# A hybrid convolution and pooling layer on one core: 32 rows moved ahead of a late product, one more pair by seven products, small products in twos, loads of the gate stage reordered

## The chip, the cores and the metric

The kernel runs on one core of a Trainium2 chip. The metric is device microseconds (us) of one execution; a result is the median of several runs. Where a profile is shown, it is of one more execution, whose own time stands beside it.

## The reference

One layer of a streaming encoder (`DEPTH` is 1) works on 2048 prompt frames of one stream and on 32 sample frames that continue another, each of 1024 numbers:

```python
hn = rmsnorm(h, g_mix)
hA, bA, cA, zA, vB, zB = split(hn @ w_in)            # six groups of 512 columns
u = cA * hA
yA = bA * (causal width-3 convolution of u + conv_b) * silu(zA)
pooled = trailing mean over 2, 4, 8 or 16 frames of vB, minus vB
yB = (pooled @ pool_w, per group of 128) * pool_scale * silu(zB)
h = h + concat(yA, yB) @ w_out
gate = sigmoid(rmsnorm(h, g_ple) @ w_ple_gate)
h = h + (p @ w_ple) * gate
return rmsnorm(h, g_final), ...                      # and the states that end each stream
```

All inputs are float32. `w_in` is 1024x3072, `w_out` and `w_ple_gate` are 1024x1024, `p` has 256 numbers a frame. The sample frames take the stream's cached states as history.

## The kernel before

**Products.** Every large operand is split in two parts, a rounded one and the rest (`split`, L81 on ScalarE and L84 on VectorE), and a product takes three matmuls for each of its contraction blocks. The three large matrix products are done as a 2x2 scheme with seven block products in place of eight: the sources of one side are summed to `11`, `12`, `S1` to `S4`, `22`, those of the other to `11`, `21`, `T1` to `T4`, `22`. One block product is 12 matmuls of 128x512 on TensorE (PE). Its banks in PSUM are named `x`, `y` and `z`: `x` gathers the products `11`, `S2`, `S3` and, as the last, the one with `T4`. `carry` copies a bank's state between, `out` adds it to the result.

**First stage: units.** The projection runs in two groups (`gi`) of two blocks of 512 frames, and four units (`j`) of 128 columns of each of the six kinds. The first unit is `Unit.plain`: it does all six kinds block by block, with whole projections (`project`, L646) of 24 matmuls for a kind and a block. While it runs, the frames of the group are normalised, turned and summed (`second`, `frame_sums`), and the seven forms are split. Six are kept in SBUF as `B0`. The seventh, `T4`, has its place in a ring of one buffer (`seventh`) that is used for something else before; so its four parts are stored to DRAM as `p_d` (`to_memory`, L546), and it is loaded back after the first unit (L1290). The other seven units (`Unit.seven`) each run three pairs of kinds, (zb, v), (c, h), (za, b), by `pair`: it takes its weights from `pair_weights`, which sums and splits them product by product, and does the seven products with `half_product`. Between the products of a unit one step of an `aside` is taken: in the first group the frame sums of the next group, in the second group the turning of `p` (`turn_p`), the 32 sample frames (`new_frames`) and the weights of the embedding (`ple_weights`). `new_frames` goes through 24 parts of `w_in`, loads two ahead, and takes one part a step: 8 matmuls of 128x256 with 32 rows (L1147).

**Second stage: output rows.** Products `p @ w_ple` of the first tiles (`embed`, tile `e`) fill the time until the weights are there. Then `w_out` is applied to pairs of tiles of 128 rows, `o0`, `o2` to `o14`, by `seven`, whose steps 1 to 6 between the products run other work: in `o0` the table `LATER` prepares the late weights (`T3`, `21`, `22`, `T4`) and frames. `h_ops` (L1315) adds the rows of `x`; `done_h` stores the sum as `h_d` and takes its squares. The 32 sample rows are a tile of their own, done by `plain` with its packed products (L337, L340), named `ol`. They stand behind `o4`. `scale_gate` scales the gate's weights on the way.

**Third stage: gate.** The rest of the embedding (`rest_e`, with frames `pps` that `load_pps` loads) runs first, with the preparation of the first pair `prep_g(0)` as steps. Then pairs `g0` to `g12` and `last_pair` (14) run by `seven`. `prep_g(i)` gives two steps that prepare the pair `i` inside the pair before. `first` loads the upper tile by rows and the lower tile by quarters (`by_quarters`, L1541) and transposes the latter on VectorE (`turned_here`, L1547). `second` transposes the upper tile on PE (`turned`: copies `ho` by ScalarE at L1530, transposes `pth` at L1532), then sums and splits. `gate_ops` (L1558 to L1570) copies, adds, takes the sigmoid and updates `h`. `done_g` (L1577, L1578) scales the finished rows and stores them.

**Order.** A planner puts each engine's instructions in order beforehand, by its own estimate of when operands and buffers are there, and each engine then runs its list in that order. `keep_in_program_order` (also `in_turn`, `pin`) holds an instruction at its place in the source; `issue_after` holds a load behind another instruction. Loads and stores are issued by SP, GpSimd (POOL) and ScalarE, each in order, so a load that waits for a buffer holds up those behind it in its queue.

Of the kernel before, what the change touches and what calls it, by code (L numbers as in the profile page):

```python
# [9 lines left out]
F32 = mybir.dt.float32  # L10
F32R = mybir.dt.float32r
# [4 lines left out]
P = 128  # L16
# [20 lines left out]
def trunk(ctx, tc, x_p, x_s, c_conv, c_pool, p_p, p_s, g_mix, w_in, conv_w, conv_b, pool_w,  # L37
# [361 lines left out]
    with ExitStack() as s1:  # L399
# [197 lines left out]
        def pair_weights(gi, ka, kb, j, name, ring, s_ring, ring_b, pin):  # L597
# [17 lines left out]
            else:  # L615
# [220 lines left out]
        class Unit:  # L836
# [65 lines left out]
            def plain(self):  # L902
# [29 lines left out]
                for b in blocks:  # L932
# [3 lines left out]
                    if b:  # L936
                        next(second)
                wza = weights("za", j, f"za{tag}")
                for b in blocks:
                    z = self.cols(V, b)  # L940
                    nc.scalar.activation(z, product_of("za", b, wza), AF.Silu)
                    c = self.cols(c_s, b)
                    nc.vector.tensor_tensor(c, c, z, op=ALU.mult)
                    if b:
                        next(second)
                wb = weights("b", j, f"b{tag}")
                for b in blocks:
                    ps = product_of("b", b, wb)
                    y = self.cols(c_s, b)
                    nc.vector.tensor_tensor(y, ps, y, op=ALU.mult)  # L950
                    self.store(j, b, c_s)


            def pair(self, ka, kb, B, D, done, ring, s_ring=None, pin=False):
# [6 lines left out]
                make = pair_weights(self.gi, ka, kb, self.j, name, ring, s_ring, pool_ring if ka == "zb" else ring, pin)  # L961
                yield
# [9 lines left out]
                half_product(X, make("11"), B["11"], True)  # L972
# [21 lines left out]
            def seven(self, B, aside, both=False):  # L994
# [27 lines left out]
                za = [self.cols(V, b) for b in range(2)]  # L1022
                gb = self.cols(U, 0)

                def za_done(b):
                    nc.scalar.activation(za[b], za[b], AF.Silu)
                    mul(self.cols(c_s, b), self.cols(c_s, b), za[b])

                def b_second():
                    mul(self.cols(c_s, 1), self.cols(c_s, 1), gb)  # L1030
                    self.store(j, 1, c_s)

                def b_first(ps):
                    mul(self.cols(c_s, 0), ps, self.cols(c_s, 0))
                    self.store(j, 0, c_s)

# [6 lines left out]
                    ("za", "b", B, {(0, 0): za[0], (0, 1): za[1], (1, 1): gb},  # L1043
                     {(0, 0): lambda ps: za_done(0), (0, 1): lambda ps: (za_done(1), b_second()), (1, 1): nothing,
                      (1, 0): b_first})]
# [67 lines left out]
        def new_frames():  # L1113
# [186 lines left out]
    with ExitStack() as s2:  # L1300
# [118 lines left out]
        W["21"] = halves(seventh("wo_21"))  # L1419

# [11 lines left out]
        hold = []  # L1432

# [34 lines left out]
        for i in range(0, NT - 1, 2):  # L1468
# [365 lines left out]
```

## Time and profile before

| | us |
|---|---|
| runs | 932.33, 930.13, 931.91 (median 931.91) |
| the profiled execution | 929.11 |
| its span, first to last instruction | 927.3 |
| PE busy | 902.0 (97%) |
| VectorE (DVE) busy | 697.1 (75%) |
| ScalarE (ACT) busy | 458.5 (49%) |
| GpSimd (POOL) busy | 158.9 (17%) |
| mean granted clock of TensorE | 0.994 |

The stages, by PE's timeline: the first unit until 90, the other units until 531.7, the first embedding until 550.9, the output tiles until 716.2, the second embedding until 742.6, the gate's pairs until 917.8, and then the last rows until the end.

How the rows are read: a timeline's row has its start in the span, its length, the engine, the line of the source, the operation, the tiles written and read, shapes, and how often it stands there in a row; in brackets the engine's idle time before it and what ended that. A row of windows has the busy time and the instructions of PE, its weight loads, DVE, ACT and POOL, then the granted clock, the busy share of the DMA engines and GB/s. A row of DMA issues has the queue, the count, the size of one and the median us from issue to landing. Matmuls overlap, so a row of several ends a little after the next one begins; the distance of starts is the pace.

### The profile page before, as it was taken

How to read it: one execution, taken by the hardware profiler on the slowest of the kernel's cores; microseconds unless marked ns; L12 is line 12 of the kernel's file. 1: busy time of each engine (PE TensorE's matmuls, PEld its weight loads, DVE VectorE, ACT ScalarE, POOL GpSimd, SP SyncE). 2: the span in 40 equal slices, each digit the busy share in tenths (PEclk: the TensorE clock that was granted, in tenths of full speed). 3: DMA queues.
4: the chain of work that ended last, by engine and by line, in shares of the span. 5: the costliest groups of instructions: out<-in, count | busy, mean ns of one | idle time of the engine just before them, and what ended most of it. 6: DMA issues, size and time to landing. Idle time of an engine off the chain costs nothing. (4 is left out here: it accounts for less than half of the span.)

```text
span 927.3 us, 12203 instructions
## 1 busy us (share of the span) xinstructions
PE 902.0 (97%) x4186; PEld 723.5 (78%) x4186; DVE 697.1 (75%) x1148; ACT 458.5 (49%) x828; POOL 158.9 (17%) x309
## 2 busy tenths in 40 slices
PE   8999999999999999999999998999999999999995
PEld 6788888878888788766688886878888778778885
DVE  6895789797993687746668679765655988888884
ACT  7752555465453354523344376434434965555553
POOL 2200121122121122100010021111111311121212
PEclk9999999999999999999999999999999999999998
DMA  8164396747599675777743695867768876476652
GB/s 277 47 206 169 104 270 188 227 153 235 174 339 428 165 226 177 246 219 236 235 145 131 225 320 166 264 224 238 223 220 276 306 249 193 165 227 206 218 186 105
DMA packets 113243, 199.56 MB, mean 215 GB/s; under 512 B 13206, under 2 KB 69950, under 8 KB 112157
## 3 DMA queue, kind: packets, MB, share of 16 engines
q1 hardware_dynamic: 88733, 117.19, 40.4%
q0 software_dynamic: 22000, 77.21, 24.6%
q10 hardware_dynamic: 2448, 4.39, 1.3%
q8 instruction: 33, 0.54, 0.2%
q14 instruction: 29, 0.24, 0.1%
HBM read 133.06 MB, written 65.67 MB: 214 GB/s over the span
## 5 line engine op out<-in xcount | busy, mean ns | idle before, releaser
L185 PE MATMUL x_o<-wo,y 128*128 128x512 f32 x192 | 47.1, 400 | 3.4 <-DVE x L1315 3.4
L185 PE MATMUL z_g<-wg,g_S 128*128 128x512 f32 x192 | 47.4, 393 | 0.7 <-ACT c_g L1558 0.7
L185 PE MATMUL z_o<-wo,y_S 128*128 128x512 f32 x192 | 47.4, 389 | 0.0
L185 PEld LDWEIGHTS x_o<-wo,y 128*128 128x128 f32 x192 | 37.1, 194 | 11.8 <-issue 3.8
L185 PE MATMUL x_o<-wo_T,y_S 128*128 128x512 f32 x192 | 46.2, 390 | 0.0
L185 PEld LDWEIGHTS z_g<-wg,g_S 128*128 128x128 f32 x192 | 35.5, 188 | 8.5 <-ACT c_g L1558 1.3
L646 PE MATMUL z_ch<-B,w_ch_S 128*128 128x512 f32 x168 | 40.8, 392 | 1.2 <-ACT U L966 1.2
L185 PEld LDWEIGHTS z_o<-wo,y_S 128*128 128x128 f32 x192 | 36.0, 188 | 7.5
L185 PEld LDWEIGHTS x_o<-wo_T,y_S 128*128 128x128 f32 x192 | 35.9, 188 | 7.6 <-DVE c_o L1315 0.2
L646 PE MATMUL x_ch<-B,w_ch_S 128*128 128x512 f32 x168 | 41.8, 392 | 0.0
L646 PE MATMUL x_zab<-B,w_zab_S 128*128 128x512 f32 x168 | 40.9, 392 | 0.2 <-DVE w_zab_S L84 0.2
L646 PE MATMUL z_zab<-B,w_zab_S 128*128 128x512 f32 x168 | 41.1, 392 | 0.0
L646 PE MATMUL x_zbv<-B,w_zbv_S 128*128 128x512 f32 x168 | 40.8, 391 | 0.0
L646 PE MATMUL z_zbv<-B,w_zbv_S 128*128 128x512 f32 x168 | 40.7, 391 | 0.0
L646 PEld LDWEIGHTS z_ch<-B,w_ch_S 128*128 128x128 f32 x168 | 31.3, 188 | 8.9 <-ACT U L966 1.6
L646 PEld LDWEIGHTS x_zab<-B,w_zab_S 128*128 128x128 f32 x168 | 31.3, 188 | 7.9 <-issue 0.8
L646 PEld LDWEIGHTS x_zbv<-B,w_zbv_S 128*128 128x128 f32 x168 | 31.3, 188 | 7.7 <-issue 0.8
L646 PEld LDWEIGHTS z_zab<-B,w_zab_S 128*128 128x128 f32 x168 | 31.2, 188 | 7.5 <-issue 0.8
L646 PEld LDWEIGHTS x_ch<-B,w_ch_S 128*128 128x128 f32 x168 | 31.3, 188 | 7.3 <-issue 0.8
L646 PEld LDWEIGHTS z_zbv<-B,w_zbv_S 128*128 128x128 f32 x168 | 31.3, 188 | 7.2 <-issue 0.8
L1577 DVE SCALAR_TENSOR_TENSOR h<-h,rstd_f,g_bc 128x1024 f32<-128x1024 f32 (+1 forms) x15 | 19.3, 1284 | 14.6 <-POOL rstd_f L77 13.0
L94 ACT ACTIVATE junk<-x 128x1024 bf16<-128x1024 f32 (+1 forms) x17 | 18.0, 1056 | 22.6 <-DVE x L1315 21.1
(561 smaller groups left out, 2297.9 us busy)
## 6 DMA issues: line engine op xcount, KB each, us to landing
wn<-in_w_in_dram SPq DMA_DIRECT2D x24, 512.0 KB, 3.8
p_dT<-T POOLq DMA_DIRECT2D x16, 512.0 KB, 5.2
y<-y_d SPq DMA_DIRECT2D x16, 512.0 KB, 5.9
h<-h_d POOLq DMA_DIRECT2D x16, 512.0 KB, 5.1
e<-e_d SPq DMA_DIRECT2D x15, 512.0 KB, 4.7
x<-in_x_prompt_dram SPq DMA_DIRECT2D x14, 512.0 KB, 4.0
out_dram<-h POOLq DMA_DIRECT2D x14, 512.0 KB, 3.4
B<-p_d POOLq DMA_DIRECT2D x3, 2048.0 KB, 15.7
```

Source lines behind the costliest of these rows:

```text
L94: ins = nc.scalar.activation(junk[:n], x[:n], AF.Square, accum_out=ssq[:n])
L185: nc.tensor.matmul(ps[:n], lhs[:, k, a, :n], w[b][:, k], start=start and k + q == 0, stop=k == KH - 1 and q == 2, skip_group_check=True)
L646: nc.tensor.matmul(ps, lhs[:, k, x], b[:, k, y], start=start and k + q == 0, stop=stop and k == KH - 1 and q == 2, skip_group_check=True)
L1577: nc.vector.scalar_tensor_tensor(h[:n], h[:n], rf[:n], g_bc[:n], op0=ALU.mult, op1=ALU.mult)
```

## The change

It has these parts:

- *The first unit's third pair.* `Unit.plain` does (za, b) by `pair`, with the sums of the group's frames, in place of four whole projections. The part that tells what is done with the results is now `third`. `T4` is loaded by POOL right after `h`. `pair_weights` stores the sums of the first group's other units for the second group, as before, and none for this unit.
- *The new rows.* `new_frames` loads four parts ahead, waits two steps longer, and takes two parts every second step.
- *The 32 output rows.* `ol` runs at step 6 of `o0`, ahead of the product with `T4`; its frames (`short_y`) and rows (`short_x`) are loaded before `o0`.
- *The gate stage.* The quarters of tile 1 (`first_lower`) are loaded before the embedding's weights; the first two `pps` use another ring (`ss`); the first pair's transpose on VectorE is pinned (its steps stay behind the same embedding tiles); `second` of the pairs 2 and 8 runs a step later; loads of `h` and stores of finished rows go to SP's queue from tile 6 on, and in the last pair.

```diff
@@ pair_weights
-                if gi == 0:
+                if gi == 0 and j:
                     kept[ka, j] = k1, k3 = ...
@@ Unit.plain
                     self.conv(b)
-                    if b:
-                        next(second)
-                wza = weights("za", j, f"za{tag}")
-                for b in blocks:
-                    z = self.cols(V, b)
-                    nc.scalar.activation(z, product_of("za", b, wza), AF.Silu)
...
-                wb = weights("b", j, f"b{tag}")
-                for b in blocks:
-                    ps = product_of("b", b, wb)
...
+                    if b == 0:
+                        steps = self.pair(*self.third(B0), raw_ring, None, True)
+                        next(steps)
+                    next(second)
+                B0["T4"] = piece_of(seventh("B0_T4"), 0)
+                nc.gpsimd.dma_start(B0["T4"].bitcast(F32), p_d["T4"])
+                p_d["T4"] = tc.dram_tile([P, KH, 2, NB], F32, name="p_dT4b")
+                for _ in steps:
+                    pass
+
+            def third(self, B):
...
+                return ("za", "b", B, {(0, 0): za[0], (0, 1): za[1], (1, 1): gb},
+                        {(0, 0): lambda ps: za_done(0), (0, 1): lambda ps: (za_done(1), b_second()), (1, 1): lambda ps: None,
+                         (1, 0): b_first})
@@ Unit.pair
+                upper = make("11") if pin and self.gi == 0 else None
                 yield
...
-                half_product(X, make("11"), B["11"], True)
+                half_product(X, upper or make("11"), B["11"], True)
@@ new_frames
-            loaded = [load(0), load(1)]
+            loaded = [load(i) for i in range(4)]
+            yield
+            yield
             yield
...
-                if i + 2 < len(order):
-                    loaded.append(load(i + 2))
+                if i % 2 == 0:
+                    continue
+                loaded.extend(load(n) for n in (i + 3, i + 4) if n < len(order))
...
+                yield
                 yield
@@ units
                     u.plain()
-                    B0["T4"] = piece_of(seventh("B0_T4"), 0)
-                    nc.sync.dma_start(B0["T4"].bitcast(F32), p_d["T4"])
-                    p_d["T4"] = tc.dram_tile([P, KH, 2, NB], F32, name="p_dT4b")
@@ output rows
+        short_y = qa.tile([P, KC, DEC], F32, tag="q", name="short_y")
+        with tc.issue_after(loaded[0]):
+            nc.sync.dma_start(short_y, y_d[:, :, SEQ:].rearrange("k p t -> p k t"))
...
+        short_a = short("yl", (short_y[:, :KH], short_y[:, KH:]), DEC)
...
+        def short_tile():
+            plain("ol", short_a, W, last_n, *h_ops([short_x], last_n, "ol", two=True))
+
-        LATER = {1: third, 2: left, 3: right, 4: later("T4", 2)}
+        LATER = {1: third, 2: left, 3: right, 4: later("T4", 2), 6: short_tile}
+        short_x = load_rows(xh, "x", NT - 1, x_p, x_s)
...
-            last = i == 4
-            if last:
-                n = tiles[NT - 1][1]
-                A = short("yl", load_y(NT - 1, n), n)
+            if i == 0:
+                done_h(NT - 1, short_x)
...
-            if last:
-                x = load_rows(xh, "x", NT - 1, x_p, x_s)
-                plain("ol", A, W, n, *h_ops([x], n, "ol", two=True))
-                done_h(NT - 1, x)
@@ gate stage
+        first_lower = by_quarters(1)
...
-        got = {0: load_pps(st.tile([P, 2, 2, P], F32R, tag="t", name=f"pps_{EARLY}"), EARLY, nc.sync)}
+        got = {0: load_pps(ss.tile([P, 2, 2, P], F32R, tag="s", name=f"pps_{EARLY}"), EARLY, nc.sync)}
...
-        got[1] = st.tile([P, 2, 2, P], F32R, tag="t", name=f"pps_{EARLY + 1}")
+        got[1] = ss.tile([P, 2, 2, P], F32R, tag="s", name=f"pps_{EARLY + 1}")
...
+        def turned_here(t, pin=False):
+            ins = nc.vector.transpose(t, t)
+            if pin:
+                tc.keep_in_program_order(ins)
...
-            nc.gpsimd.dma_start(rows_of(y_p, y_s, r, n), h[:n])
+            (nc.sync if 6 <= i < NT - 1 else nc.gpsimd).dma_start(rows_of(y_p, y_s, r, n), h[:n])
@@ last_pair
-            h = [load_rows(xh, "h", i + b, h_d, queue=nc.gpsimd) for b in range(2)]
+            h = [load_rows(xh, "h", i + b, h_d) for b in range(2)]
...
-                (nc.scalar if b else nc.gpsimd).dma_start(y[:, cut:], o[:, cut:])
+                (nc.scalar if b else nc.sync).dma_start(y[:, cut:], o[:, cut:])
@@ prep_g and the loop over the gate's pairs
-                got["lower"] = by_quarters(i + 1)
+                got["lower"] = by_quarters(i + 1) if i else first_lower
...
-            return {2: first, 3: second}
+            return {2: first, 4 if i in (2, 8) else 3: second}
...
-                steps[2 if c == 2 else 3]()
+                steps[c // 2 + 1]()
...
-            h = [load_rows(xh, "h", i + b, h_d, queue=nc.gpsimd) for b in range(2)]
+            h = [load_rows(xh, "h", i + b, h_d, queue=nc.gpsimd if i < 6 else nc.sync) for b in range(2)]
```

More of the change, by code (lines that the diff above doesn't have):

```diff
@@ L1498, in trunk, with by_quarters @@
         weight_parts(W, tops, None, "11", "T1")
+        def by_quarters(i):
+            r, n = tiles[i]
+            t = ring4(ya, f"hn_{i}")
+            for q in range(4):
+                nc.sync.dma_start(t[q * 32:q * 32 + 32].rearrange("p (g c) -> p g c", g=4),
+                                  h_d[r:r + P, q * 256:q * 256 + 256].rearrange("(g p) c -> p g c", p=32))
+            return t
+        first_lower = by_quarters(1)
         shared = slot("wq")
         wp = [[shared[:, (2 * k + h) * D:(2 * k + h + 1) * D] for h in range(2)] for k in range(2)]
-        got = {0: load_pps(st.tile([P, 2, 2, P], F32R, tag="t", name=f"pps_{EARLY}"), EARLY, nc.sync)}
+        got = {0: load_pps(ss.tile([P, 2, 2, P], F32R, tag="s", name=f"pps_{EARLY}"), EARLY, nc.sync)}
         for k in range(2):
@@ L1534, in turned @@
             return out
-        def by_quarters(i):
-            r, n = tiles[i]
-            t = ring4(ya, f"hn_{i}")
-            for q in range(4):
-                nc.sync.dma_start(t[q * 32:q * 32 + 32].rearrange("p (g c) -> p g c", g=4),
-                                  h_d[r:r + P, q * 256:q * 256 + 256].rearrange("(g p) c -> p g c", p=32))
-            return t
-        def turned_here(t):
-            nc.vector.transpose(t, t)
+        def turned_here(t, pin=False):
+            ins = nc.vector.transpose(t, t)
+            if pin:
+                tc.keep_in_program_order(ins)
             u = t.rearrange("p (g k t) -> p k g t", g=4, k=KC)
@@ L1742, in first @@
                     load()
-                lower.extend(turned_here(got["lower"]))
+                lower.extend(turned_here(got["lower"], not i))
             def second():
```

36 lines of the change are left out of this document (15 added, 21 removed).

## The prediction

> **What bounds the kernel now.** First I read the page's busy shares, then the list of what TensorE (PE) waits for, then PE's timeline around each place that the change touches, each time with the other engines' timelines beside it.
>
> ```profile
> PE 902.0 (97%) x4186; PEld 723.5 (78%) x4186; DVE 697.1 (75%) x1148; ACT 458.5 (49%) x828; POOL 158.9 (17%) x309
> ```
>
> PE works 902.0 of the span's 927.3 us. So time goes only where PE has fewer matmuls, runs them faster, or waits less. The single largest wait inside it is this:
>
> ```profile
> PE x_o L185 <- DVE x L1315: 3.4, 1, 3.4
> ...
> PE pth L1532 <- ACT ho L1530: 1.8, 2, 1.2
> PE e L109 <- DMA pps<-pp_d: 1.6, 1, 1.6
> ```
>
> (the columns are total, times, longest). The change works on all three of these and takes matmuls away in two places. I cost its four parts in order of time. The profiled execution took 929.11 us, 2.80 under the median of the runs (931.91); the parts are summed against the profile, and the sum is then taken from the median.
>
> **Part A: the first unit's third pair by seven products.** Before, `za` and `b` are four full projections of 24 matmuls:
>
> ```profile
> 68.22 11.04 PE L646 MATMUL za<-B,w_za 128*128 128x512 f32 x48
> 79.10 11.04 PE L646 MATMUL b<-B,w_b 128*128 128x512 f32 x48
> 89.98 2.88 PE L646 MATMUL x_zbv<-B,w_zbv 128*128 128x512 f32 x12
> ```
>
> From 68.22 to 89.98 stand 96 matmuls in 21.76 us, 0.2267 each (a product of 12 is 2.72). Seven products are 84: −2.72. The weight sums that this adds are DVE's, which has room there (third busy column):
>
> ```profile
> 80.00:84.00 4.00, 4.00 (x19) 3.32 (x18) 2.65 (x5) 0.41 (x1) 0.00 (x0) 1.00 0.29 109
> 84.00:88.00 4.00, 4.00 (x20) 3.30 (x19) 0.69 (x1) 0.54 (x1) 0.00 (x0) 1.00 0.24 88
> ```
>
> In the changed order only the second product's weights come late, by an estimated 0.2 from the number of pieces (0.6 to 0.7 each) ahead of them in DVE's queue.
>
> The new wait is the seventh product's frames, `T4`. They are split, stored to DRAM by POOL in four parts, and loaded back as one. Before, the load was needed only by the next unit's seventh product; now PE wants it after 72 of the pair's matmuls and 2 of the next unit, at 68.22 + 74 × 0.2267 + 0.2 = 85.2.
>
> ```profile
> 71.28 0.68 DVE L84 TENSOR_TENSOR T<-f,T 128x512 fp32r<-128x512 f32 x1
> ```
>
> ```profile
> 72.25 0.84 POOL L546 DMA_DIRECT2D p_dT<-T  x1 [9.63 <-DVE T L84]
> ```
>
> ```profile
> B_T<-p_dT SPq DMA_DIRECT2D x1, 2048.0 KB, 8.5
> ...
> p_dT<-T POOLq DMA_DIRECT2D x1, 512.0 KB, 4.2
> ```
>
> ```profile
> B<-p_d POOLq DMA_DIRECT2D x3, 2048.0 KB, 15.7
> ```
>
> The last part is stored at 72.25, right behind its split. In the changed order two more splits stand ahead of it on DVE (0.6 each by the steps of that queue), so the store goes out at 73.45 and lands at 77.65 (4.2). The load then takes 8.5 by the row of the same load before; the other row, 15.7, is of 2 MB loads that were queued seven at once on POOL, and is the far end. So `T4` lands at 86.2, and PE waits 1.0 (bounds: 0, and 93.4 − 85.2 = 8.2). I take 8.5, because it is the same transfer at nearly the same time. A = −2.72 + 0.2 + 1.0 = −1.5; the bounds are −2.5 and +5.7, or +7.6 with the slow clock that part B shows behind a long wait. The Trainium skill's "DMA: Bandwidth & Descriptors" (section "Anatomy of one DMA — SWDGE (gpsimd) path") fits such a transfer as 2.0 us plus bytes over 436 GB/s, an estimate of 6.8 for 2 MB, with which there would be no wait and the sum would be 1.0 better; no row here shows a 2 MB load that fast.
>
> **Part B: the 32 rows before the late product.** The short tile stood behind `o4`; now it stands inside `o0`, before the product of `A22` with `T4`.
>
> ```profile
> 567.50 0.61 PE L185 MATMUL x_o<-wo,y 128*128 128x512 f32 x2
> 571.53 6.88 PE L185 MATMUL x_o<-wo,y 128*128 128x512 f32 x22 [3.42 <-DVE x L1315]
> ```
>
> ```profile
> 570.71 0.68 DVE L1315 TENSOR_TENSOR x<-x_o,x 128x512 f32<-128x512 f32 x1
> ```
>
> ```profile
> 572.00:574.00 2.00, 2.00 (x6) 1.54 (x6) 2.00 (x4) 0.72 (x1) 0.52 (x1) 0.55 0.87 203
> 574.00:576.00 2.00, 2.00 (x7) 1.54 (x6) 1.84 (x4) 1.93 (x5) 1.08 (x2) 0.59 0.97 274
> ```
>
> ```profile
> 722.00:726.00 4.00, 2.42 (x15) 1.91 (x14) 3.93 (x8) 4.00 (x10) 2.09 (x3) 1.00 1.00 379
> ```
>
> PE does two matmuls of the next tile and then waits for DVE to empty the bank (done at 571.39). Behind the wait the granted clock (the third number from the end) is 0.55 and 0.59, with 6 and 7 matmuls in 2 us where 0.2267 each makes 9. The last row is a stretch with a shorter wait, of 1.57 (part D): its clock is 1.00. The 24 matmuls from 567.50 end at 571.53 + 6.71 = 578.24: 10.74 where 24 × 0.2267 = 5.44 are due, so 5.30 are lost, 3.42 waiting and the rest to the clock. The Trainium skill's "TensorE: Matmul & The Clock Gate" (Part 1) says that a window of about 3.4 us idle halves the clock until one such window was busy: with that a stall well under 3.4 costs only itself. The trace agrees on both sides, half the clock after 3.42 and all of it after 1.57; so I price short stalls at their length, and long ones like this one.
>
> ```profile
> 613.66 1.08 PE L337 MATMUL x_ol<-wo,yl_a 128*64 128x512 f32 x4
> ...
> 621.02 1.32 PE L185 MATMUL x_o<-wo,y 128*128 128x512 f32 x5
> ```
>
> The short tile costs 7.36 in either place. In the changed order 24 of its 32 matmuls (5.5 us) stand between `S4` and the late product, which PE so reaches at 573.0. DVE gets to the sum at 571.39 plus two small splits of the short rows (0.5): 571.9, 1.1 early. The short tile's last eight matmuls wait for a DVE sum that I place at 574.3, when PE is there at 574.4. Its frames are loaded behind the lower weight rows and split by DVE some 10 us after, and the load of `o2`'s rows, which now waits for a store of `o0`'s rows, has some 5 us in hand; these are estimates from the queues' orders and the durations of such rows. B = −5.3, −5.1 with 0.2 for that tight step; if DVE were late by its own queue, part of the 3.42 would stay, so −3 at the worst.
>
> **Part C: the new rows' products two at a time.** 24 groups of 8 small matmuls stand between the big products of the second half. Before, most stand alone:
>
> ```profile
> 396.05 1.07 PE L1147 MATMUL new<-wn,xs 128*32 128x256 f32 x16
> 397.05 3.06 PE L646 MATMUL x_zbv<-B,w_zbv 128*128 128x512 f32 x12
> 400.04 0.64 PE L1147 MATMUL new<-wn,xs 128*32 128x256 f32 x8
> 400.60 3.02 PE L646 MATMUL y_zbv<-B,w_zbv 128*128 128x512 f32 x12
> 403.56 0.64 PE L1147 MATMUL new<-wn,xs 128*32 128x256 f32 x8
> ```
>
> A pair of groups and a product take 400.04 − 396.05 = 3.99, so the pair costs 1.27; a single and a product take 403.56 − 400.04 = 3.52, so the single costs 0.80. Before there are 18 singles and 3 pairs, 18.2 us; the changed order has 12 pairs, 15.2. C = −3.0, and I see no reason for a gain beyond it; if the saving came only from the switch at one side, half would be left (−1.5).
>
> ```profile
> wn<-in_w_in_dram SPq DMA_DIRECT2D x24, 512.0 KB, 3.8
> ```
>
> The weight rows (3.8 us to land) are now loaded four ahead and two per two steps, so each has over 6 us. The steps behind them move by two products, 5.4 us; what they make is used only by the embedding, when the units are over: hidden.
>
> **Part D: the gate stage.** Loads are moved ahead, so PE's wait for the embedding's frames goes:
>
> ```profile
> 724.30 16.60 PE L109 MATMUL e<-wq,pps 128*128 128x512 f32 x72 [1.57 <-DMA pps<-pp_d]
> ...
> 752.15 1.18 PE L1532 MATMUL pth<-ident,ho 128*128 128x128 f32 x8 [1.22 <-ACT ho L1530]
> ...
> 759.52 3.01 PE L185 MATMUL z_g<-wg,g_S 128*128 128x512 f32 x12 [0.73 <-ACT c_g L1558]
> ```
>
> ```profile
> 751.48 1.14 ACT L1530 COPY ho<-hn 128x512 f32<-128x512 f32 x2 [4.01 <-DMA hn<-h_d]
> ```
>
> −1.6 in the embedding. Then `g0` has less room. Before, ACT waited 4.01 for the upper rows of the next pair, and PE lost 1.22 + 0.73 = 1.95. In the changed ACT order the copies of these rows stand ahead of the copy that frees `g0`'s first bank for the third product. That product ended at 752.15 − 1.22 = 750.9, so it began at 748.2, and would begin at 746.6 now that PE is 1.6 earlier. If the rows land as late as before (751.48), PE waits 6 us with the copies. The quarters of the lower tile are loaded earlier, so less is ahead of these rows; I place the landing in the middle, at 748, and with the two copies (1.14) and the bank's (0.5) the wait is 3.0 against 1.95: +1.0 (bounds −2 and +4). The second wait on `ho` (1.8 − 1.2 = 0.6 in the list above) goes with the transposes moved by a step, and I give back half for new tight places: −0.3. D = −1.6 + 1.0 − 0.3 = −0.9.
>
> The later pairs take a new risk. From tile 6 on, the output stores go to SP's queue, which issues in order, and there they stand ahead of the load of the next upper rows. That load so waits for DVE's last scaling:
>
> ```profile
> 860.93 1.28 DVE L1577 SCALAR_TENSOR_TENSOR h<-h,rstd_f,g_bc 128x1024 f32<-128x1024 f32 x1 [0.71 <-POOL rstd_f L77]
> ```
>
> ```profile
> 864.87 1.18 PE L1532 MATMUL pth<-ident,ho 128*128 128x128 f32 x8
> ```
>
> ```profile
> e<-e_d SPq DMA_DIRECT2D x5, 512.0 KB, 5.9
> ```
>
> By these times the store goes at 862.2, the load at 862.8, lands by 5.9 at 868.7, and the copy ends 0.57 later, at 869.3. PE's transposes stood at 864.87; the changed order has them later by half a product and 11 matmuls, at 864.87 + 1.36 + 2.49 = 868.7. So 0 to 0.6 in each of two pairs; I take none of it for the sum.
>
> **The sum.** −1.5 − 5.1 − 3.0 − 0.9 = −10.5: 918.6 for an execution like the profiled one, and 931.91 − 10.5 = 921.4 for the median.
>
> **The rivals.**
> - *T4 lands late* (0.12). For it: 2 MB loads took 15.7. Against: that was a queue of seven. A then is +7.6 instead of −1.5, 930.5 in all.
> - *The upper rows behind the stores come late, no slow clock* (0.12). Two pairs lose some 1.7 each where the load takes 7 instead of 5.9: 924.8. For it: the load is the first that waits for this scaling. Against: the transposes were moved back with it.
> - *The same with the slow clock, slower than before* (0.07). If in `g6`, `g8` and `g10` the rows come over 3.4 us late, each costs what part B's wait cost, 5.3 less 0.2: 921.4 + 15.3 = 936.7. This decides from a landing of about 9 us; the 5.9 above is against it, the DMA share of 1.00 at 722 (the last number but one of that row) is for it, if the pairs see such a load again.
> - *T4 in time and `g0` without a new wait* (0.07): 1.0 + 2.0 better, 918.4; for it, DMA is at 0.24 to 0.29 of its share from 80 to 88, against it, it is the 8.5 of the one row. The skill's figure for a load would give the first of these.
> - *It does not do what it says*: the built program shows the order of its instructions, seven products and twelve pairs among them, so only times are open.
>
> **How the numbers follow.** The forecast holds 0.62, with 917.5 to 925 as its own range. With the cases beside it the range is 917.5 to 928.5; outside lie the slower case, half of the late `T4`, and a little at the low end. About 0.3% (2.8 us) is what a measurement of this kernel can tell from no change: the bounds are 929.1 and 934.7. Faster: 0.62 + 0.12 + 0.07 + half of 0.12 = 0.87; same: the other half, 0.06; slower: 0.07.
>
> **What would show it.** A: PE's `x_zab` product with `T4` right behind `z_zab`, with a wait near 1. B: no wait on x_o, the clock at 1.00 from 564 to 580. C: 12 rows of 16 `new` matmuls. D: no wait on `pps`, and a wait of some 3 in `g0`'s first block. I am wrong if the waits on `B_T`, `ho` or `hn` sum to more than 8 us, or if B's lost 5.3 reappears at another product of `o0` or `o2`.

## The result, and the profile after

The changed kernel took 920.0 us (median of 4 runs, 917.26 to 922.09) against 932.12 for the kernel before (930.13 to 932.85): a ratio of 0.9872, with a 95% interval of 0.9839 to 0.9904. The forecast was 921.4 with a range of 917.5 to 928.5, so the time is right. The profiled execution took 917.26, the fastest of the four, with a span of 915.5, and it shows that two of the four terms were not: A brought nothing, and D far more than its 0.9.

The page's busy shares, and then the list of PE's waits, of the changed kernel:

```profile
PE 895.3 (98%) x4174; PEld 722.7 (79%) x4174; DVE 702.6 (77%) x1158; ACT 460.3 (50%) x834; POOL 151.6 (17%) x291
```

```profile
PE gm L447 <- DMA gm_row<-in_g_mix_dram: 2.3, 1, 2.3
PE x_zab L646 <- DMA B_T<-p_dT: 2.3, 1, 2.3
PE e L109 <- DMA wq<-wl_d: 1.6, 1, 1.6
```

PE has 12 matmuls less, and 6.7 us less of busy time. The wait on `x_o` is gone from the list, and so are both on `ho`. In their place stands a wait of 2.3 on `T4` (`B_T`), and the wait at the second embedding is as long as before but on another transfer: `wq`, not `pps` (in eight other profiles with the same loads at this place it was shorter, 0.3 to 1.2).

The stages tell more than the list. From the starts of the same products in both timelines of PE:

| stretch | before | after | difference | predicted |
|---|---|---|---|---|
| start to the first unit's third pair | 68.22 | 68.75 | +0.5 | 0 |
| that pair, and the next unit's first product (A) | 24.48 | 24.45 | 0.0 | −1.5 |
| units from there to the new rows | 296.28 | 297.46 | +1.2 | 0 |
| new rows, to the units' end (C) | 142.73 | 139.64 | −3.1 | −3.0 |
| first embedding | 19.19 | 19.20 | 0.0 | 0 |
| output tiles (B) | 165.34 | 160.48 | −4.9 | −5.1 |
| second embedding (D) | 26.34 | 26.43 | +0.1 | −1.6 |
| `g0`, to `g2`'s second product (D) | 25.24 | 22.70 | −2.5 | +1.0 |
| later pairs, to the last embedding (D) | 143.98 | 142.70 | −1.3 | −0.3 |
| to the last matmul's end | 5.94 | 5.95 | 0.0 | 0 |
| from there to the end of the span (D) | 9.56 | 7.74 | −1.8 | 0 |

B and C are as worked out. In B the short tile stands where the wait stood, and PE's timeline runs through:

```profile
566.56 1.08 PE L337 MATMUL x_ol<-wo,yl_a 128*64 128x512 f32 x4
...
572.09 1.54 PE L185 MATMUL x_o<-wo,y 128*128 128x512 f32 x6
573.47 1.08 PE L337 MATMUL x_ol<-wo,yl_a 128*64 128x512 f32 x4
574.39 1.09 PE L340 MATMUL x_ol<-wo,yl_a 128*32 128x512 f32 x4
575.31 4.26 PE L185 MATMUL x_o<-wo,y 128*128 128x512 f32 x18
```

From 566.56 to 572.09 are the 5.53 that cover DVE's sum, and PE goes on without a wait; the clock is 1.00 in all windows from 564 to 580, of which this is one (busy time and count of PE, PEld, DVE, ACT, POOL, then clock, DMA share, GB/s):

```profile
572.00:576.00 4.00, 4.00 (x19) 2.71 (x18) 3.88 (x7) 1.15 (x2) 1.35 (x2) 1.00 0.89 274
```

For C, two rows of the same timeline:

```profile
396.93 1.07 PE L1149 MATMUL new<-wn,xs 128*32 128x256 f32 x16
...
403.64 1.07 PE L1149 MATMUL new<-wn,xs 128*32 128x256 f32 x16
```

A pair and two products take 403.64 − 396.93 = 6.71, which is 1.27 for the pair. The prediction's 1.27 held to the digit, and 12 such rows stand in the timeline.

In A the wait is there, more than twice as long as priced:

```profile
85.22 0.61 PE L646 MATMUL x_zbv<-B,w_zbv 128*128 128x512 f32 x2
88.11 2.98 PE L646 MATMUL x_zab<-B_T,w_zab 128*128 128x512 f32 x12 [2.28 <-DMA B_T<-p_dT]
```

and so the 2.7 us of twelve matmuls are given back on the spot.

### The profile page after: what moved, and what is told of

It reads as the page before. It is cut to its first block, busy times and chain, and to the rows that moved or that the text cites. A ratio compares the mean times of both kernels' runs of the same rounds, so it can differ in the third digit from the quotient of the medians.

```text
span 915.5 us, 12179 instructions
## 1 busy us (share of the span) xinstructions
PE 895.3 (98%) x4174; PEld 722.7 (79%) x4174; DVE 702.6 (77%) x1158; ACT 460.3 (50%) x834; POOL 151.6 (17%) x291
## 4 chain that ended last, share of the span: by engine, by line
PE 65%; DMA 7%; issue 5%; DVE 2%; ACT 1%; POOL 1%; SPq 0%; POOLq 0%; DVEq 0%; ACTq 0%
PE x_g L185 9%; PE x_o L185 9%; PE x_zab L646 5%; PE z_g L185 5%; PE e L109 4%; PE x_zbv L646 4%; PE x_ch L646 4%; PE z_o L185 4%; DMA raw_zab_0b<-in_w_in_dram 4%; PE z_zab L646 2%; PE y_g L185 2%; PE y_o L185 2%; PE z_ch L646 2%; PE z_zbv L646 2%; DMA B<-p_d 2%
## 5 line engine op out<-in xcount | busy, mean ns | idle before, releaser
L646 PE MATMUL x_zab<-B,w_zab_S 128*128 128x512 f32 x192 | 46.9, 392 | 0.6 <-ACT V L983 0.4
L646 PE MATMUL z_zab<-B,w_zab_S 128*128 128x512 f32 x192 | 46.7, 390 | 0.0
L185 PE MATMUL x_o<-wo,y 128*128 128x512 f32 x192 | 45.2, 389 | 0.0
L646 PEld LDWEIGHTS x_zab<-B,w_zab_S 128*128 128x128 f32 x192 | 35.7, 188 | 9.6 <-ACT V L983 0.8
L646 PEld LDWEIGHTS z_zab<-B,w_zab_S 128*128 128x128 f32 x192 | 35.8, 188 | 7.8 <-DVE w_zab_S L84 0.3
L81 ACT CAST y_S<-y_fS 128x512 fp32r<-128x512 f32 x28 | 17.0, 620 | 27.2 <-PE x_o L185 11.5
L1316 DVE TENSOR_TENSOR c_o<-x_o,x 128x512 f32<-128x512 f32 x14 | 9.7, 690 | 21.9 <-PE x_o L185 21.8
```

The costliest lines, as they stand in the source:

```text
L81: ins = nc.scalar.copy(hi, src)
L185: nc.tensor.matmul(ps[:n], lhs[:, k, a, :n], w[b][:, k], start=start and k + q == 0, stop=k == KH - 1 and q == 2, skip_group_check=True)
L646: nc.tensor.matmul(ps, lhs[:, k, x], b[:, k, y], start=start and k + q == 0, stop=stop and k == KH - 1 and q == 2, skip_group_check=True)
L1316: add = lambda o, a, b: nc.vector.tensor_tensor(o, a, b, op=ALU.add)
```

## The experiments

Twelve kernels ran. One is the changed kernel again. In four, one part each is undone in the changed kernel; the others take apart A and D. The ratios are to the kernel before on the same chip; they are worked out from all runs, so they need not be the quotient of two medians.

| kernel | median us | ratio | 95% interval |
|---|---|---|---|
| changed (two sets of runs) | 920.0, 918.67 | 0.9872, 0.9857 | 0.9839 to 0.9904, 0.9836 to 0.9879 |
| without A | 915.98 | 0.9826 | 0.9807 to 0.9845 |
| without B | 923.73 | 0.9906 | 0.9888 to 0.9925 |
| without C | 923.82 | 0.9907 | 0.9887 to 0.9926 |
| without D | 928.45 | 0.9967 | 0.9947 to 0.9987 |
| T4 loaded alone | 917.63 | 0.9848 | 0.9827 to 0.9870 |
| wq ahead of half of wg_b | 918.62 | 0.9858 | 0.9838 to 0.9878 |
| one last store on POOL | 919.35 | 0.9861 | 0.9842 to 0.9880 |
| T4's product put off | 916.12 | 0.9841 | 0.9822 to 0.9860 |
| the same, and wq ahead | 915.44 | 0.9826 | 0.9810 to 0.9841 |
| without A, wq ahead | 915.62 | 0.9844 | 0.9819 to 0.9868 |
| stores and loads on POOL | 918.79 | 0.9866 | 0.9850 to 0.9882 |

**The changed kernel again.**

> The changed kernel once more, so that the next three are compared with it on one chip: ratio 0.987, between 0.984 and 0.990. The first four experiments are read again with it.

918.67, a ratio of 0.9857: this is the one that the others are compared with below, where nothing else is said.

**Without A.** The first unit as before, all else as changed:

```diff
-                    if b == 0:
-                        steps = self.pair(*self.third(B0), raw_ring, None, True)
...
+                wza = weights("za", j, f"za{tag}")
+                for b in blocks:
+                    z = self.cols(V, b)
+                    nc.scalar.activation(z, product_of("za", b, wza), AF.Silu)
...
+                    nc.sync.dma_start(B0["T4"].bitcast(F32), p_d["T4"])
```

> The changed kernel without part A: the first unit's third pair is done by four whole projections again, and T4 is loaded on SP's queue behind them. Theory (from the two profiles): the 12 matmuls saved (2.7 us) are given back by the wait for T4 (2.3 us) and by some 0.2 for late weights, and about 1 us of short waits in the units behind comes from the other order that the planner makes. So A is worth nothing or costs up to 1 us: this kernel is 0 to 1 us faster than the changed one, a ratio of 0.986 to 0.988 to the kernel before. Rival (the prediction's sum): A is worth 1.5 us, so this kernel is 1.5 us slower than the changed one, 0.989. In the profile the theory expects no wait on B_T, the pair from za to the next unit's y_zbv product 24.5 us long as in both, and the waits on ACT V and ACT zs in the units gone.

0.9826: the kernel without A is faster than the changed one, by 2.7 us beside the second set of its runs (915.49 to 918.01 against 917.15 to 922.09 in both sets together). Four of its five runs are below all eight of the changed kernel, though the intervals of the ratios overlap. In the profile the pair and the next product take 24.48 (the changed kernel 24.45), and the units behind 296.98, where kernels with A have 297.46 and 298.54. The waits on `ACT V` and `ACT zs` did not go as expected; the first stayed (0.57), the second is not in the list. So A costs, and by the medians more than the theory said. The rival, A worth 1.5, is out.

**Without B.**

```diff
-        LATER = {1: third, 2: left, 3: right, 4: later("T4", 2), 6: short_tile}
+        LATER = {1: third, 2: left, 3: right, 4: later("T4", 2)}
...
+                plain("ol", A, W, n, *h_ops([x], n, "ol", two=True))
```

> The changed kernel without part B: the 32 output rows stand behind o4 again. Theory and prediction agree: 5 us slower than the changed kernel (4.9 by the profiles' starts of the gate stage, 5.1 predicted), a wait of 3.4 us on x_o behind DVE in o0, and a granted clock near 0.55 for some 3.4 us behind it. Rival: the wait depends on how far DVE's queue was behind by chance of the order, and with the other parts in place it is under 2 us, with the clock at 1.00 behind it, so 2 us or less.

0.9906, 3.7 to 5.1 us slower than the changed kernel's two medians. PE's timeline has the old wait, to the digit, and the windows behind it the slow clock:

```profile
571.05 6.84 PE L185 MATMUL x_o<-wo,y 128*128 128x512 f32 x22 [3.42 <-DVE x L1316]
```

```profile
572.00:574.00 2.00, 2.00 (x6) 1.56 (x5) 2.00 (x5) 1.15 (x2) 0.05 (x1) 0.50 0.92 200
574.00:576.00 2.00, 2.00 (x9) 1.64 (x8) 1.56 (x3) 1.70 (x4) 1.07 (x2) 0.84 0.73 232
```

So the wait came again at its full length with the other parts in place, as the order of DVE's work in `o0` has it, and the rival falls. In this execution the output tiles took 167.62, 7.1 more than in the changed kernel's, with two more short waits of 0.5 behind `c_o`; the medians say less.

**Without C.**

```diff
-            loaded = [load(i) for i in range(4)]
+            loaded = [load(0), load(1)]
...
-                if i % 2 == 0:
-                    continue
```

> The changed kernel without part C: the new rows' products one group a step again. Theory and prediction agree: 3.0 us slower than the changed kernel (3.1 by the profiles), all of it between the first and the last of these products, 0.33 for each of the 9 pairs that fall apart. Rival: what the profile shows there is partly the planner's different order around it, and the loss is half, 1.5 us.

0.9907, and in the profile the stretch from the new rows to the units' end takes 142.76 against 139.64: 3.1, in the place that was named. Shown, and the rival is out. The medians differ by more, 3.8 to 5.2; the profiled execution, 920.86, is the fastest of the six, and where the others lose the rest is not shown.

**Without D.** The whole gate stage as before.

> The changed kernel with the whole gate stage as before (part D undone). Theory (from the two profiles): 5 to 5.5 us slower than the changed kernel: g0 gets its two waits back (2.5 with what hangs on them), the later pairs theirs (1.2), the end its 1.8, and the embedding's start is no different (its wait is on pps instead of on wq, 1.6 in both). Rival (the prediction's sum): D is worth 0.9 us, and what the profiles show beyond it belongs to the luck of the executions. In the profile the theory expects the time from the last matmul's end to the end of the span at 9.5, against 8.6 in the changed one or less.

0.9967: 8.5 to 9.8 us slower than the changed kernel by the medians. By the profile's stretches: the second embedding 26.38 (no difference, as expected), `g0` 26.55 against 22.70 (+3.9), the later pairs 144.48 against 142.70 (+1.8), the end 9.60 against 7.74 (+1.9): 7.5, and D is the largest part, not the smallest; the rival's 0.9 is out. The smaller changes of D (the rings of `pps`, the early quarters, the later transposes) were not undone one by one. The `g0` term is larger than the 2.5 of the kernel before, for a reason that the timeline and two windows show:

```profile
751.07 1.97 PE L1537 MATMUL pth<-ident,ho 128*128 128x128 f32 x8 [2.10 <-ACT ho L1535]
```

```profile
750.00:752.00 2.00, 0.93 (x5) 0.93 (x6) 1.20 (x2) 1.59 (x3) 0.53 (x1) 0.74 1.02 414
752.00:754.00 2.00, 2.00 (x8) 1.81 (x7) 0.40 (x1) 1.99 (x4) 0.00 (x0) 0.50 1.04 346
```

The wait was 2.10 and the clock went to 0.50 behind it. That a stall of this length can do it was not in the prediction.

**T4 loaded alone.** The next unit's weights for c and h wait until `T4` has landed:

```diff
             raw_loads.append(queue.dma_start(t, w_in[:, col:col + P].rearrange("(k p) n -> p k n", p=P)))
+            if t4_load and j == 1 and kind in ("c", "h"):
+                tc.add_manual_dep(raw_loads[-1].ins, t4_load[0].ins.name, ...)
```

> The changed kernel, with the next unit's two weight loads (c and h, 512 KB each) held until T4 has landed. In the changed kernel's profile these and two stores of 256 KB move in the same stretch as T4's 2 MB, whose load takes 9.7 us. Theory (T4 shares the bandwidth): alone it takes 7 to 7.5 us, so PE's wait on B_T falls from 2.3 to 0.2 or less, and the kernel gets up to 2 us faster, if the held weights are not late in turn (they are wanted by PE some 20 us later). Rival (the pace is that of the queue or of the round trip through DRAM, whatever moves beside it): the load still takes 8.5 or more, the wait stays over 1, and the time does not change by more than 0.5.

The DMA issues of the changed kernel around it, and of this one:

```profile
B_T<-p_dT POOLq DMA_DIRECT2D x1, 2048.0 KB, 9.7
```

```profile
B_T<-p_dT POOLq DMA_DIRECT2D x1, 2048.0 KB, 9.0
```

9.0 instead of 9.7, and the wait 1.6 instead of 2.3. The two loads beside it are worth 0.7 us. Two stores of 256 KB still run beside it, and what of the 9.0 they make was not taken apart. The theory's 7 to 7.5 is wrong. The pair gained 0.7 to 0.8; that execution lost 3.0 in a wait of `z_o` on `c_o` at 668, so its time can't be read for it, and the medians don't tell it from the changed kernel. The clock stayed at 1.00 behind that wait of 3.0.

**wq ahead of half of wg_b.**

```diff
-            bots = rows_of_weight(cmb, "wg_b", g_d, 1)[0]
+            bots = rows_of_weight(cmb, "wg_b", g_d, 1, range(2))[0]
+        with tc.issue_after(wq_last.ins):
+            bots += rows_of_weight(cmb, "wg_b", g_d, 1, range(2, KH))[0]
```

> The changed kernel, with the last two of the four lower rows of the gate's weights (512 KB each) loaded behind the embedding's weights (wq) and not ahead of them. Theory (the early loads of part D only swapped one wait for another: wq is now behind 1 MB more at the full rate of some 400 GB/s): the wait on wq at the embedding's start, 1.6, falls by 1 to 1.6 us, and the weight sums on DVE come 2.5 us later, which g0 has in hand. So 1 us faster. Rival: the waits only move again, the embedding's start gains and g0's first products wait on T2 or on ho by as much: no change.

The wait is gone from the list, and the second embedding takes 24.62 instead of 26.43 and 26.04 in the two profiles of the changed kernel; `g0` takes 22.95 instead of 22.70. So the early loads of `wg_b` had in fact pushed `wq` back, and the exchange is undone at the price of 0.25: in the profile, 1.2 to 1.6 us. (Seven other profiles without the exchange have 25.1 to 25.9 there, so the gain may be as little as 0.2.) The median shows nothing of it (918.62 against 918.67). A reason is seen at `T4`, in this execution's timeline and windows:

```profile
88.08 4.49 PE L646 MATMUL x_zab<-B_T,w_zab 128*128 128x512 f32 x12 [2.44 <-DMA B_T<-p_dT]
```

```profile
88.00:90.00 2.00, 1.93 (x5) 1.57 (x6) 0.00 (x0) 0.00 (x0) 0.00 (x0) 0.50 0.64 212
90.00:92.00 2.00, 2.00 (x8) 1.58 (x7) 1.77 (x3) 0.00 (x0) 0.00 (x0) 0.67 0.14 53
```

and in those of the changed kernel, with almost the same wait:

```profile
88.00:90.00 2.00, 1.89 (x8) 1.61 (x9) 0.00 (x0) 0.00 (x0) 0.00 (x0) 1.00 0.64 211
90.00:92.00 2.00, 2.00 (x10) 1.66 (x9) 1.55 (x3) 0.00 (x0) 0.00 (x0) 1.00 0.03 12
```

Behind a wait of 2.44 the clock is halved and the twelve matmuls take 4.33 (92.41 − 88.08); behind 2.28 they take 2.83. Over the nine profiles of kernels that wait for `T4` at this place, the clock was halved behind 2.27, 2.40, 2.44 and 2.82, and stayed full behind 1.58, 2.18, 2.26, 2.28 and 2.37. The pair takes 26.0 to 26.6 with it and 24.3 to 24.6 without (23.75 where `T4` was loaded alone). The same wait, to a hundredth, went either way. The other executions have no timeline, but their mean granted clock points the same way: 0.994 to 0.998 in the five of this kernel, 0.997 or 0.998 in all ten of the two kernels below that have no wait for `T4`.

**T4's product put off.** Part A stays, but its last product runs behind the next unit's first two:

```diff
-                for _ in steps:
-                    pass
+                for _ in range(6):
+                    next(steps)
+                put_off.append(steps)
...
                     next(steps[i])
+                    if put_off and (i, s) == (0, 2):
+                        for _ in put_off.pop():
+                            pass
```

> The changed kernel with part A kept, but its seventh product put off: it runs behind the next unit's first two products, 5.4 us later, at about 90.7, when T4 landed at 88 in all profiles so far. Theory (A's 2.7 us are there and the wait for T4 takes them back, 2.3 to 2.8 us, and in some executions another 1.7 to 2.2 because the clock is halved behind it): no wait on B_T, clock at 1.00, and the stretch from the pair's start to the next unit's second product grows no longer than 24.45 less 2.3 for the same number of matmuls. So 2.5 us faster than the changed kernel, up to 4 where that had the slow clock, and as fast as the one without part A or 1 us faster. Rival (what makes A worthless lies in the units behind it, whose order the planner changes): the waits on ACT V, ACT zs and ACT U in the next units grow by what is saved here, and nothing is gained against the changed kernel.

PE's timeline has no wait there any more:

```profile
85.09 2.88 PE L647 MATMUL x_zbv<-B,w_zbv 128*128 128x512 f32 x12
87.81 2.88 PE L647 MATMUL y_zbv<-B,w_zbv 128*128 128x512 f32 x12
90.53 2.89 PE L647 MATMUL x_zab<-B_T,w_zab 128*128 128x512 f32 x12
```

From the pair's start to the new rows this kernel takes 320.60, the changed one 321.91 and 323.11 in its two profiles, the one without A 321.46. The next kernel, with the product put off too, takes 320.64. So the wait was what ate A's saving, and putting the product off brings 1.3 to 2.5. It doesn't bring all: against the kernel without A only 0.9 of the 2.7 is left. The waits of PE in the stretch sum to 4.0 here and to 2.9 there (on `ACT U` 1.6 against 1.2, on `ACT V` 0.9 against 0.6, on `ACT zs` 0.6 against none), which is 1.1 of the 1.8 that are missing; the rest was not taken apart. The rival holds for that part, though these waits are not A's alone: the other kernel without A has 0.7 on `ACT zs`. 916.12 against 918.67: faster, though the intervals of the two ratios overlap.

**The same, and wq ahead.**

> The one before, and the last two lower rows of the gate's weights behind wq, as tried alone. Theory: both savings add, 2.5 and 1.4: some 4 us faster than the changed kernel, ratio near 0.982, the fastest of all if the kernel without part A does not gain more by the same. Rival: the second saving is lost again in g0, as the time of that kernel alone (no faster than the changed one) could mean, then 0.984.

915.44, 0.9826 (0.9810 to 0.9841), runs from 914.39 to 915.91, and with the two kernels without A (915.98 and 915.62) the fastest here; they can't be told apart. Against the changed kernel that is 3.2 to 4.6 us. The second embedding took 24.53, where the one before it had 25.09 with a wait on `wq` of only 0.3 in its execution.

**Without A, wq ahead.**

> The changed kernel without part A and with the last two lower rows behind wq. Theory: the kernel without A (0.9826) less 0.7 for the wait on wq that it had left, ratio 0.982. Rival: no gain over 0.9826, since its wait was only 0.7 and DVE's sums come later.

915.62 against 915.98, not to be told apart: five of six runs lay between 915.03 and 916.83, and the profiled one at 922.33, with a wait of 3.0 of `x_o` on `c_o` in a late output tile (at 698) and slow matmuls behind it (a clock of 0.73 from 700 to 704). The wait on `wq` was 0.6 in that execution, so the change of order didn't even do its part there. Inconclusive.

**One last store on POOL.**

```diff
-                (nc.scalar if b else nc.sync).dma_start(y[:, cut:], o[:, cut:])
+                (nc.scalar if b else nc.gpsimd).dma_start(y[:, cut:], o[:, cut:])
```

> The changed kernel, with one single DMA back on its old queue: the smaller part of the first tile's last store goes out on POOL, as before. Theory: this issue is the only thing on POOL near the end, and with it the time from the last matmul's end to the end of the span goes from 7.7 back to 9.6, 1.9 us slower, with everything ahead of it unchanged. Rival: the end is shorter because of the other stores and loads that went from POOL to SP in the last pairs, and this one makes no difference.

From the last matmul's end to the end of the span it took 7.85, the changed kernel 7.74 and 7.72: the rival holds, this store alone is worth 0.1 and not 1.9.

**Stores and loads on POOL.**

```diff
-            (nc.sync if 6 <= i < NT - 1 else nc.gpsimd).dma_start(rows_of(y_p, y_s, r, n), h[:n])
+            nc.gpsimd.dma_start(rows_of(y_p, y_s, r, n), h[:n])
...
-            h = [load_rows(xh, "h", i + b, h_d) for b in range(2)]
+            h = [load_rows(xh, "h", i + b, h_d, queue=nc.gpsimd) for b in range(2)]
...
-            h = [load_rows(xh, "h", i + b, h_d, queue=nc.gpsimd if i < 6 else nc.sync) for b in range(2)]
+            h = [load_rows(xh, "h", i + b, h_d, queue=nc.gpsimd) for b in range(2)]
```

> The changed kernel with the loads of h and the stores of finished rows from tile 6 on, and the last pair's loads of h, back on POOL's queue, and the one last store still on SP (its move alone made no difference to the end). Theory: the end of the span grows again from 7.7 to 9.5 behind the last matmul, since what costs there is POOL's last transfers in the final pair and not the very last store: 1.8 us slower, and g8 to g14 are otherwise unchanged or lose less than 0.5. Rival (SP's in-order queue costs the pairs something, as the prediction's risk had it): the pairs get 0.5 to 1.5 faster and make good a part of the 1.8.

The end takes 9.52, and the pairs 142.61 against 142.70. So the 1.8 us at the end come with the rows' transfers on POOL's queue from tile 6 on, and SP's in-order queue costs the pairs nothing. The medians don't show it (918.79 against 918.67, where 1.8 more was expected); it is read from the profile alone. There the last store goes out 3.1 us behind the last matmul's end, as in the changed kernel; what takes longer is behind it:

```profile
907.00 4.74 SPq L1651 DMA_DIRECT2D out_dram<-hg  x2
```

The second of these two is issued at 907.00 + 4.74 − 0.34 = 911.40, and the span ends at 917.8, 6.4 later. In the changed kernel the same store goes out at 910.89 and the span ends 4.6 later. None of the transfers on POOL is near: their last one in the final pair was at 898.51, nine microseconds before the last matmul. What is longer is POOL's closing instruction, a DRAIN, which the timelines leave out (count; shortest, median and longest in ns; first and last start). Here and in the changed kernel:

```profile
L1838 POOLq DRAIN  x3: 46/97/6497, 910.2 to 917.5; - x3
```

```profile
L1838 POOLq DRAIN  x3: 46/98/5028, 909.7 to 915.2; - x3
```

The long one ends at 916.7 here and at 914.7 there, behind SP's last wait (914.6 and 914.0), and the span ends 1.1 and 0.8 later. Its length goes with the number of transfers that POOL has issued in the whole program: 5.03 us in the ten profiles with 148 or 149, 5.11 with the one store more of the run before this, 6.50 here with 18 more, 6.58 in the kernel without D with 19 more and in the kernel before. So each of the moved transfers costs 0.08 us at the end, and 18 of them make 1.5 of the 1.8. Why it does is not shown.

## Why the prediction was right, and where it was not

*B and C* are right by their own steps: the cover of 5.5, DVE's place (its sum is done at 570.5, 1.6 before PE is there), the clock that stays full, the twelve pairs at 1.27. Both undoings show it.

*A's sign was wrong.* Three steps failed. The load of `T4` was priced at 8.5, the row of the same load on SP's queue; on POOL's, where it now is, it takes 9.7 (9.6 to 10.4 in ten profiles), 9.0 with little beside it. A load on SP's queue at this place was not tried, so how much of that is the queue is not shown. The store before it went out at 73.90 and the load at 78.27, 0.6 later than worked out; but PE got there 0.6 later too, at 85.83, so it is the load that made the wait 2.3 and not 1.0. The next step priced a short wait at its length, with the 1.57 us wait and its full clock as the witness. Its rule, a window of about 3.4 us, was the one of the Trainium skill's page "TensorE: Matmul & The Clock Gate" (Part 1). One witness was too few: a wait of some 2.3 cost its own length in four of eight profiles, and some 4.0 in the other four. The Trainium skill's page "TensorE: Matmul & The Clock Gate" (Part 1) also says that the window runs free, so that what a burst of work gets varies from run to run; the trace agrees in so far as the same wait went both ways, while the reading that a wait must be near 3.4 to halve the clock does not hold here (2.27 and 2.40 did it). Last, the units behind were put at 0 and lost some 0.9: kernels with A take 296.7 to 298.6 from the next unit's second product to the new rows (nine profiles, those with the product put off left out, in the mean 297.8), and 296.28, 296.98 and 297.53 without A (296.9), so the two overlap, and what the planner's other order has to do with it is not shown. By the medians A costs 2.7 to 4.0 us as it stands. The stretch from the pair's start to the new rows takes 321.0 to 324.5 in the nine profiles with A and 320.8 to 322.0 in the three without, 1.6 apart in the mean, and the longest three are of those with the halved clock; where the rest of the medians' difference lies is not shown.

The estimate of 6.8 for 2 MB, from the Trainium skill's page "DMA: Bandwidth & Descriptors" ("Anatomy of one DMA — SWDGE (gpsimd) path"), is out: 8.1 to 10.4 in the profiles here.

*D was sized too small.* The embedding's −1.6 did not come. The step that failed moved `wg_b` ahead and looked at `pps` only; `wq` had to wait for its buffer, and then came behind the 2 MB of `wg_b`. DMA was at its full rate before (a share of 0.98 to 1.00 from 710 to 730) and after (1.00 to 1.03 from 695 to 715), and the wait changed its name. `g0`'s +1.0 was −2.5. There the landing of the next pair's upper rows was put at 748, in the middle of its bounds, with the moved quarters alone in mind. But the step before it failed: SP's loads of that pair's rows, quarters first, wait for buffers that DVE's sums of `wg_b` free (the quarters waited 8.3 us for that before, 1.3 after), and with `wg_b` early those sums came early too. The sums and the issue of the upper rows, before:

```profile
740.68 2.49 DVE L1776 TENSOR_TENSOR wg_b<-wg_b,wg_t 128x512 f32<-128x512 f32 x4
```

```profile
743.35 1.07 SPq L396 DMA_DIRECT2D hn<-h_d  x1
```

The same in the changed kernel, with ScalarE's copy:

```profile
732.56 1.89 DVE L1784 TENSOR_TENSOR wg_b<-wg_b,wg_t 128x512 f32<-128x512 f32 x3
```

```profile
733.32 0.34 SPq L396 DMA_DIRECT2D hn<-h_d  x1
```

```profile
738.80 0.61 ACT L1545 COPY ho<-hn 128x512 f32<-128x512 f32 x1
```

The load goes out 10.0 us earlier, of which 6.2 are the whole stage's (`g0` begins at 736.41, not 742.58); the copy comes 12.7 us earlier than before (751.48) and waits for nothing, and `g0` has no wait. The early loads paid, but one stage later than where they were meant to. The later pairs gained 1.3 where I had given half back, and SP's stores ahead of the loads cost nothing that the run with POOL's queue shows. The end's −1.8 was not seen at all: the tail was put at 0 because its own work is unchanged, while it also pays for the transfers that POOL has issued before.

The sum of −10.5 against −11.85 by the profiles came out because A's loss and the units' (1.5 and 1.2 over the forecast) and D's gain (4.6 over it) lie on opposite sides. That it came so near is luck.

*The rivals.* A late `T4` was named with the right place; its wait was 1.2 to 1.8 longer than priced, in every profile but the one where it was loaded alone, and not 8; the clock came with it in four of nine. The rows behind the stores were not late in the changed kernel's two profiles; waits of 0.2 and 0.6 on `ho`, in a late pair of two other kernels with D, are all that came.

## What to carry to other kernels

Where the loads are moved, redo the whole chain that hangs on them: here a load that went out 10 us earlier, 3.9 of them gained on its own stage, was worth more than the wait that the change aimed at, and that wait only passed to the next transfer in the same full queue. Work that is saved ahead of a DMA round trip is saved only if the consumer has other work in the meantime; putting off one product by two took the wait away. A queue can cost at the very end for what was issued on it long before. And a wait of two microseconds on TensorE is to be priced with a chance of the slow clock behind it, not at its length alone.

## What the runs showed of the hardware that was not expected

- The clock fell to 0.50 behind waits of 2.10 to 2.82, in four of the eight profiles where a wait of over 2 us stood before the same product, and there is no length between 2.2 and 2.4 at which it decides (halved behind 2.27, full behind 2.28 and 2.37). Behind two waits of 3.0 in output tiles it was 1.00 once (668) and 0.73 once (698).
- A load of 2 MB on POOL's queue took 9.0 us with little beside it and 9.6 to 10.4 with two loads more; on SP's, a few us later in the program, it took 8.1 to 8.5 in three profiles.
- The end of the span came 1.8 us later when 18 transfers of rows from tile 6 on went on POOL's queue and not on SP's, though none of them was near the end and the last stores were the same: POOL's closing DRAIN took 6.50 in place of 5.03, 0.08 for each; one single store on POOL cost 0.08 there.
- Waits of 3.0 in an output tile (`c_o`) came in two single executions, at 668 and 698, of kernels that share their output stage with others that had none. Both end the same chain: ScalarE, in order, stood before the scaling of the gate's weights (`gs`), 3.5 us for a store and 9.0 us for a load of them, and its split of `y_S` behind that held DVE (7.7 and 8.7 us), which had the sum for `c_o` behind it. Why these transfers were late is not shown.
